# S5 input products in a two-layer hybrid encoder: two groups per weight load, against a block-diagonal operand

## The chip, the core and the metric

The kernel is one program on one core of a Trainium2 chip. The metric is device time in microseconds (us). Engines are named as in the profile: PE (TensorE's matmuls), PEld (its weight loads), DVE (VectorE), ACT (ScalarE), POOL (GpSimd), SP (the engine that issues nearly all DMAs).

## The reference

`x` is [1, 256, 1024] in float32. Each of two layers runs a half-step FFN, a mixer of three gated branches, and another half-step FFN. The change lies in the S5 branch of the mixer. Cut to that:

```
u = (h @ w_in)[..., :512]          # 256 tokens, 32 groups of 16 channels
b_bar = ((lam_bar - 1) / lam) * b  # complex, [group, 64 states, 16 channels]
bu = einsum('blgh,gph->blgp', u, b_bar)
states = scan(a*s + bu), forward and, with its own tables, backward
y = real(einsum('blgp,ghp->blgh', states, c)) + d_skip * u
y_s5 = gelu(y) * sigmoid(gelu(y) @ w_glu)
```

The other two branches are gated linear attention (GLA) and grouped-query attention. Their weighted sum goes through `w_out` and is added to `x`.

## The kernel before

**The large products.** Every weight matrix streams through `load` and `stream`: SP brings 256 rows by 512 columns (`raw`), ACT casts them to a high part (`hi`, L209), DVE subtracts to get the low part (`lo`, L210), and PE does three products per tile of 128 by 128 activations (`mm3`, L219 to L221, each 512 columns wide, tile `mm`). Four `hi` and four `lo` buffers rotate, so ACT and DVE may run at most that far ahead of PE.

**S5.** The recurrence is worked over chunks of four tokens, so 256 tokens are 64 chunks, and a group's operand for one chunk has 4 x 16 = 64 rows. `s5` transposes `u` into `U` (L797, L798): 128 partitions hold two groups, one on partitions 0 to 63 and one on 64 to 127, and there are 16 such pairs of 64 columns. It then goes through four quarters `q` of eight groups (four pairs). For each quarter: 16 input products `S` (L818), one for each pair `a`, real or imaginary part `r`, and group `g` of the pair; eight DVE products of `S` with the rotations `e` (the loop over `g` behind L818, through `mul`, L349); one addition and one subtraction; four scans into `run` (L835, L836); products back; and the output products `yp` (L853 on `U` and `mt`, L856 on the states). A float32 matmul that isn't a transpose leaves two records in the trace, one `mm` leaves one. The input product of group `g` uses only 64 rows of the array, the lower or the upper ones, and a stationary tile `bb` of 64 x 128.

**Who sets the order.** `weave` emits steps of the main stream (`w_in`, then merge gates `g0` to `g2`, GLU `G`, branch products `b0` to `b2`, `w_out`) with steps of S5, GLA and attention between them. The scheduler then puts each engine's instructions in an order of its own, by a simulated timeline. Engines run their lists in that order. The S5 work of layer 0 lies at about 240 to 375 us of the span, that of layer 1 at about 925 to 1060 us.

**Names at the far end of the mixer.** `as` (L1070) are attention scores, `apt` (L1085) transposed probabilities, `ao` (L1092) the product with the values; `amx` (L1075) is the row maximum on DVE, L1078 the exponential on ACT, L1081 the scaling on DVE. `sp`, `kv`, `go`, `goT`, `keT` belong to GLA.

Of the kernel before, what the change touches and what calls it, by code (L numbers as in the profile page):

```python
# [9 lines left out]
F32 = mybir.dt.float32  # L10
# [28 lines left out]
# main steps before a side part begins, and its steps per main step  # L39
# [12 lines left out]
# columns of the constants: those for the mixer, then those for the tables  # L52
# [4 lines left out]
def constants():  # L57
    """Arrays that depend on shapes alone, one row per partition."""
    c = np.zeros((P, C_ALL), np.float32)
    p = np.arange(P)  # L60
    inv = (10000.0 ** (-np.arange(16, dtype=np.float32) * 2.0 / 32)).astype(np.float32)
    for t in range(NT):
        tok = t * P + p
        for blk, pos in ((0, tok // 64), (1, tok % 64)):
            ang = (pos.astype(np.float32)[:, None] * inv[None]).astype(np.float64)
            for half in range(2):
                o = t * 64 + blk * 32 + half * 16
                c[:, C_COS + o:C_COS + o + 16] = np.cos(ang)
                c[:, C_SIN + o:C_SIN + o + 16] = np.sin(ang) * (1 if half else -1)
    c[:, C_MASK:C_MASK + P] = p[:, None] < p[None]  # L70
    c[:, C_TWO:C_TWO + P] = 1 + np.eye(P)
    i = np.arange(SEQ)
    c[:, C_RST:C_RST + SEQ] = i % P != 0
    n = np.arange(64)
    c[:64, C_RM:C_RM + 64] = n != 0
    c[64:, C_RM:C_RM + 64] = n != 63
    q = p % 32
    c[p, C_DM + q] = 1.0
    c[:, C_SGN] = np.where(p < 64, 1.0, -1.0)
    return c  # L80


def cols(*parts):
    """Columns of weights [K, N] side by side: for the k tiles [a, z)."""
    def f(a, z):
        res, o = [], 0
        for w, cs in parts:
            res.append((w[a * P:z * P, cs].rearrange("(k p) n -> p k n", p=P), 0, o))
            o += cs.stop - cs.start
        return res  # L90
    return f


def weave(main, sides, up=nullcontext):
    """Emit main; from its step `start` on, `per` steps of a side part after each step of main.
    sides: list of [start, per, generator]. Whatever is left of them comes in the end."""
    acc = [0.0] * len(sides)
    for i, _ in enumerate(main):
        for j, (start, per, g) in enumerate(sides):
            if i >= start:  # L100
                acc[j] += per
                while acc[j] >= 1.0:
                    acc[j] -= 1.0
                    with up():
                        next(g, None)
    for _, _, g in sides:
        for _ in g:
            pass


def rest(*gens):
    """Emit what is left of these parts, in turn, as one step."""
# [13 lines left out]
class Enc:  # L126
# [38 lines left out]
    def vectors(self, *names, eng=None):  # L165
        """Parameters of channels, to partitions: [128 channels, (layer, tile)]"""
# [26 lines left out]
    def load(self, pieces):  # L193
        """pieces: list of (dram AP [partitions, k tiles, columns], first partition, first column)"""
# [21 lines left out]
    def mm3(self, ps, act, w, first, last):  # L216
        """act: (hi, lo) [128 k, 128 tok]; w: (hi, lo) [128 k, n]"""
# [5 lines left out]
    def stream(self, act, nk, blocks, lead=1):  # L223
        """act(k, t) -> (hi, lo). blocks: list of (pieces(k0, k1) in k tiles, width, evac(t, ps)).
        The first `lead` blocks take their first chunks together."""
# [135 lines left out]
    def cmul_steps(self, o_re, o_im, a_re, a_im, b_re, b_im, tmp, neg=False):  # L361
        """o = a * b; with neg, o_im is its negative. tmp: four scratch APs"""
# [13 lines left out]
    def horner(self, out, x, cs):  # L376
        """cs from the highest power down"""
# [6 lines left out]
    def reduce_arg(self, r, n, x, inv, parts):  # L384
        """n = nearest integer of x * inv; r = x - n * (sum of parts)"""
# [40 lines left out]
    def s5_params(self, l, c):  # L426
# [68 lines left out]
        # the first four powers, turned back by a chunk  # L495
# [12 lines left out]
        # ef: powers 0 .. 7 of the turn over a chunk; eg: those of its eighth power  # L508
# [130 lines left out]
    def small_tables(self, l, pp):  # L639
        """What the mixer needs apart from its large weights: half the GLA gain, the padded gate weights with the  # L640
        bias as a last row, the rotary tables with the gains of q and k"""
# [36 lines left out]
    def split_into(self, hi, lo, src):  # L678
        """src -> two float32r parts"""
# [68 lines left out]
    def gate_stream(self, l, i, act, rstd, gates):  # L748
        """The tanh of half the gate's argument: sigmoid(v) = (1 + tanh(v / 2)) / 2"""
# [32 lines left out]
    def s5(self, l, m):  # L782
# [7 lines left out]
        U = mp.tile([P, 16, 64], F32, name=f"U{l}", tag="U")  # L790
        run = mp.tile([P, 2, GQ * 64], F32, name=f"run{l}", tag="yT")
        edge = run.rearrange("p r (g c) -> p r g c", g=GQ)
        for a in range(2):
# [4 lines left out]
            nc.scalar.copy(U[:, a * 8:a * 8 + 8], pt)  # L798
        yield
        yg = mp.tile([P, 2, 4, 8, 16], F32, name=f"yg{l}", tag="yg")  # L800
        for q in range(NQ):
# [11 lines left out]
            S = [self.psm.tile([P, 2, 256], F32, name=self.nm("S"), tag="sm") for _ in range(2)]  # L813
            for a in range(4):
                for r in range(2):
                    for g in range(2):
                        rows = slice(g * 64, (g + 1) * 64)
                        nc.tensor.matmul(S[g][:, r, a * 64:(a + 1) * 64], bb[rows, a, r], U[rows, pair[a]],  # L818
                                         start=True, stop=True)
            yield  # L820
            flat = lambda a: a.rearrange("p g c -> p (g c)")
            t1, t2, t3, t4 = (self.t2([P, 512]) for _ in range(4))
            for g in range(2):
                cs = slice(g * 256, (g + 1) * 256)
                self.mul(t1[:, cs], e[:, 0, cs], S[g][:, 0])
                self.mul(t2[:, cs], e[:, 1, cs], S[g][:, 1])
                self.mul(t3[:, cs], e[:, 0, cs], S[g][:, 1])
                self.mul(t4[:, cs], e[:, 1, cs], S[g][:, 0])
                yield
# [3 lines left out]
            # sums up to the chunk before (forward: after), nothing at the ends  # L833
# [14 lines left out]
            for i in range(2):  # L848
                gh = [(g, h, h * 2 + i, yp[g][h * 64:(h + 1) * 64, i].rearrange("p t f -> p (t f)"))
                      for g in range(2) for h in range(2)]  # L850
                for g, h, a, o in gh:
                    rows = slice(g * 64, g * 64 + 64)
                    nc.tensor.matmul(o, U[rows, pair[a]], mt[rows, a], start=True, stop=False)  # L853
# [47 lines left out]
    # ---- gate logits: z in two parts against weights in two parts, the products one above the other:  # L901
    # ---- [high z, 1 | high z, 1 | low z] . [high w, high b | low w, low b | high w]
# [18 lines left out]
    # ---- gated linear attention, both directions, a head at a time, over chunks of 128 tokens; the exponents  # L921
# [1 line left out]
    def gla(self, l, m, y):  # L923
# [26 lines left out]
        for h in range(GH):  # L950
# [34 lines left out]
            # a token's own score is the same both ways: forward ones above the diagonal, twice those on it, backward below  # L985
# [113 lines left out]
    def branch(self, l, b, y, gates):  # L1099
        """Generator bodies run late: y[b] is there by then."""  # L1100
# [76 lines left out]
```

## Time and profile before

| | |
|---|---|
| median of 3 timed runs | 1378.79 us (1378.58 to 1380.41) |
| span of the profiled execution | 1376.2 us |
| median less that span | 2.6 us |
| PE busy | 1336.0 us, 97% |
| PEld busy | 1061.6 us, 77% |
| DVE busy | 1018.4 us, 74% |
| ACT busy | 698.6 us, 51% |
| POOL busy | 73.5 us, 5% |

The page gives the profiled execution by its span, from the first to the last instruction; a timed run has a little around it. A matmul's record runs until its result has drained, so neighbouring records overlap: what a matmul costs the stream is read as the distance from its start to the start of the next. The weight loads (PEld) lie beside the matmuls. The clock of TensorE was granted in full for nearly the whole span (mean 0.996).

### The profile page before, as it was taken

Reading aid. Unit: us, or ns where it says so; the run is one execution under the profiler, and the core shown is the slowest. Engines: PE = TensorE matmul, PEld = TensorE weight load, DVE = VectorE, ACT = ScalarE, POOL = GpSimd, SP = SyncE. Lnnn points to the kernel's source line nnn. Section 1 sums busy time; section 2 is a strip of 40 time slices with the busy share of each in tenths; the row PEclk is TensorE's granted clock in tenths of the full one; section 3 lists DMA queues with packets and bytes.
Section 4 is the critical chain, followed back from the end, with each engine's and each line's share of the span. In section 5 each row is a group of like instructions: output and inputs, shape, how many; then the busy total and the mean of one; then the engine's idle time right before and its main releaser. Section 6 shows DMA issues by size and latency. Waiting matters only on the chain.

```text
span 1376.2 us, 19506 instructions
## 1 busy us (share of the span) xinstructions
PE 1336.0 (97%) x6920; PEld 1061.6 (77%) x6920; DVE 1018.4 (74%) x1826; ACT 698.6 (51%) x1102; POOL 73.5 (5%) x104
## 2 busy tenths in 40 slices
PE   7999999999999999999999999999999999999997
PEld 5878788778787678768877777887787877888886
DVE  5899975779986789996465775457799767655553
ACT  5545345447585355445355454354475754555542
POOL 1020210000100000110000000000001000000000
PEclk9999999999999999999999999999999999999999
DMA  7766666565453366666665646566654533655662
GB/s 227 195 211 224 234 222 179 189 205 198 140 183 122 107 161 206 200 202 221 198 195 173 204 149 204 180 178 202 196 200 134 168 107 122 191 178 186 182 213 76
DMA packets 201201, 249.88 MB, mean 182 GB/s; under 512 B 40856, under 2 KB 134600, under 8 KB 201104
## 3 DMA queue, kind: packets, MB, share of 16 engines
q1 hardware_dynamic: 200496, 247.59, 57.5%
q8 instruction: 54, 0.88, 0.3%
q10 hardware_dynamic: 608, 1.06, 0.2%
q14 instruction: 43, 0.35, 0.1%
HBM read 234.44 MB, written 13.11 MB: 180 GB/s over the span
## 4 chain that ended last, share of the span: by engine, by line
PE 63%; issue 17%; DVE 13%; DMA 3%; ACT 3%; POOL 1%; SPq 0%; POOLq 0%; ACTq 0%; DVEq 0%
PE mm L220 18%; PE mm L219 17%; PE mm L221 17%; DVE lo L210 4%; PE S L818 1%; DMA raw<-in_ffn_w_gate 1%; DMA raw<-in_ffn_w_up 1%; PE as L1070 1%; ACT hi L209 1%; PE ao L1092 1%; DVE t L349 1%; PE st L298 1%; DVE run L836 1%; DVE run L835 1%; PE apt L1085 1%
## 5 line engine op out<-in xcount | busy, mean ns | idle before, releaser
L210 DVE TENSOR_TENSOR lo<-raw,hi 128x1024 fp32r<-128x1024 f32 x412 | 499.4, 1217 | 191.7 <-ACT hi L209 184.1
L209 ACT CAST hi<-raw 128x1024 fp32r<-128x1024 f32 x412 | 427.7, 1042 | 305.6 <-PE mm L221 276.3
L220 PE MATMUL mm<-lo,hTh 128*128 128x512 f32 (+1 forms) x1120 | 445.3, 398 | 5.3 <-DVE lo L210 4.9
L219 PE MATMUL mm<-hi,hTh 128*128 128x512 f32 (+1 forms) x1120 | 437.6, 396 | 2.7 <-ACT hTh L267 2.7
L221 PE MATMUL mm<-hi,hTl 128*128 128x512 f32 (+1 forms) x1120 | 436.1, 392 | 0.0
L220 PEld LDWEIGHTS mm<-lo,hTh 128*128 128x128 f32 x1120 | 211.2, 189 | 51.7 <-DVE lo L210 9.2
L219 PEld LDWEIGHTS mm<-hi,hTh 128*128 128x128 f32 x1120 | 211.2, 189 | 45.5 <-ACT hTh L267 3.8
L221 PEld LDWEIGHTS mm<-hi,hTl 128*128 128x128 f32 x1120 | 210.6, 188 | 40.6 <-DVE hTl L268 0.3
L220 PE MATMUL mm<-lo,sThffn 128*128 128x512 f32 x352 | 138.9, 395 | 2.0 <-DVE lo L210 2.0
L221 PE MATMUL mm<-hi,sTlffn 128*128 128x512 f32 x352 | 138.1, 393 | 0.0
L219 PE MATMUL mm<-hi,sThffn 128*128 128x512 f32 x352 | 136.4, 395 | 0.0
L300 ACT CAST sThffn<-st 128x256 fp32r<-128x256 f32 x88 | 32.6, 372 | 128.7 <-PE st L298 128.5
L220 PEld LDWEIGHTS mm<-lo,sThffn 128*128 128x128 f32 x352 | 66.4, 189 | 16.6 <-DVE lo L210 2.5
L221 PEld LDWEIGHTS mm<-hi,sTlffn 128*128 128x128 f32 x352 | 66.5, 189 | 14.1
L219 PEld LDWEIGHTS mm<-hi,sThffn 128*128 128x128 f32 x352 | 66.5, 189 | 13.8
L301 DVE TENSOR_TENSOR sTlffn<-st,sThffn 128x256 fp32r<-128x256 f32 x88 | 36.9, 421 | 50.3 <-ACT sThffn L300 49.9
L294 ACT ACTIVATE t<-mm,rstd 128x256 f32<-128x256 f32 x88 | 41.6, 475 | 43.0 <-PE mm L221 40.2
L295 DVE SCALAR_TENSOR_TENSOR t<-mm,rstd,t 128x256 f32<-128x256 f32 x88 | 41.4, 479 | 12.6 <-ACT t L294 12.4
L818 PEld LDWEIGHTS S<-U,bb 64*128 64x128 f32 x256 | 24.6, 187 | 12.8 <-issue 11.2
L298 PE MATMUL st<-ident,t 128*128 128x128 f32 x176 | 33.4, 272 | 0.0
L298 PEld LDWEIGHTS st<-ident,t 128*128 128x128 f32 x176 | 24.4, 140 | 11.3
L349 DVE TENSOR_TENSOR t<-e,S 128x256 f32<-128x256 f32 x64 | 22.4, 414 | 12.7 <-DMA e<-scr 6.9
(355 smaller groups left out, 1452.6 us busy)
## 6 DMA issues: line engine op xcount, KB each, us to landing
raw<-in_ffn_w_gate SPq DMA_DIRECT2D x176, 256.0 KB, 3.7
raw<-in_ffn_w_up SPq DMA_DIRECT2D x176, 256.0 KB, 4.4
raw<-in_ffn_w_down SPq DMA_DIRECT2D x88, 512.0 KB, 4.6
raw<-in_w_in SPq DMA_DIRECT2D x48, 512.0 KB, 4.4
raw<-in_w_merge_gate SPq DMA_DIRECT2D x48, 512.0 KB, 3.8
raw<-in_w_out SPq DMA_DIRECT2D x16, 512.0 KB, 4.6
scr<-e SPq DMA_DIRECT2D x6, 768.0 KB, 3.7
e<-scr SPq DMA_DIRECT2D x6, 768.0 KB, 5.7
```

The source lines that it names most:

```text
L209: nc.scalar.copy(hi[:, :e - s, :width], raw[:, :e - s, :width])
L210: nc.vector.tensor_tensor(lo[:, :e - s, :width], raw[:, :e - s, :width], hi[:, :e - s, :width].bitcast(F32), op=ALU.subtract)
L219: nc.tensor.matmul(ps, act[0], w[0], start=first, stop=False)
L220: nc.tensor.matmul(ps, act[0], w[1], start=False, stop=False)
L221: nc.tensor.matmul(ps, act[1], w[0], start=False, stop=last)
L294: nc.scalar.activation(sg, ps[:, :256], AF.Silu, scale=rstd[:, t:t + 1])
L295: nc.vector.scalar_tensor_tensor(s, ps[:, 256:], rstd[:, t:t + 1], sg, op0=ALU.mult, op1=ALU.mult)
L298: nc.tensor.transpose(pt[:, j], s[:, j * P:(j + 1) * P], self.ident)
L300: nc.scalar.copy(h, pt)
L301: nc.vector.tensor_tensor(sl[:, 2 * b:2 * b + 2, t * P:(t + 1) * P], pt, h.bitcast(F32), op=ALU.subtract)
L349: self.nc.vector.tensor_tensor(out, a, b, op=ALU.mult)
L818: nc.tensor.matmul(S[g][:, r, a * 64:(a + 1) * 64], bb[rows, a, r], U[rows, pair[a]], start=True, stop=True)
```

## The change

`U` becomes a tile of 16 x 2 x 64 columns. For each pair, column block 0 holds the lower group's operand on partitions 0 to 63 and zeros below it, block 1 the upper group's operand on partitions 64 to 127 and zeros above it. POOL writes the zeros (two instructions per layer); ACT copies each transposed half to its block (four copies per layer in the place of two). One input product now uses all 128 rows and streams 128 columns: 8 products per quarter in the place of 16. `S` is split by real and imaginary part instead of by group, so that DVE takes 512 columns in one instruction, four instructions per quarter in the place of eight. The first output product (L855 now) reads its group's block of `U`. The block of SBUF that the program reserves for descriptors written by GpSimd shrinks from the default to 1024 bytes per partition; the profile before shows no queue of that kind. Comments and docstrings are taken out, some replaced by blank lines; from the S5 function on, line numbers are larger by two or three.

```diff
-        U = mp.tile([P, 16, 64], F32, name=f"U{l}", tag="U")
+        U = mp.tile([P, 16, 2, 64], F32, name=f"U{l}", tag="U")
+        for g in range(2):
+            nc.gpsimd.memset(U[g * 64:(g + 1) * 64, :, 1 - g], 0.0)
...
-            nc.scalar.copy(U[:, a * 8:a * 8 + 8], pt)
+            for g in range(2):
+                nc.scalar.copy(U[g * 64:(g + 1) * 64, a * 8:a * 8 + 8, g], pt[g * 64:(g + 1) * 64])
...
-            S = [self.psm.tile([P, 2, 256], F32, name=self.nm("S"), tag="sm") for _ in range(2)]
-            for a in range(4):
-                for r in range(2):
-                    for g in range(2):
-                        rows = slice(g * 64, (g + 1) * 64)
-                        nc.tensor.matmul(S[g][:, r, a * 64:(a + 1) * 64], bb[rows, a, r], U[rows, pair[a]],
-                                         start=True, stop=True)
+            S = [self.psm.tile([P, 4, 2, 64], F32, name=self.nm("S"), tag="sm") for _ in range(2)]
+            for r in range(2):
+                for a in range(4):
+                    nc.tensor.matmul(S[r][:, a].rearrange("p g c -> p (g c)"), bb[:, a, r],
+                                     U[:, pair[a]].rearrange("p g c -> p (g c)"), start=True, stop=True)
...
-            for g in range(2):
-                cs = slice(g * 256, (g + 1) * 256)
-                self.mul(t1[:, cs], e[:, 0, cs], S[g][:, 0])
-                self.mul(t2[:, cs], e[:, 1, cs], S[g][:, 1])
-                self.mul(t3[:, cs], e[:, 0, cs], S[g][:, 1])
-                self.mul(t4[:, cs], e[:, 1, cs], S[g][:, 0])
-                yield
+            gac = lambda x: x.rearrange("p (g a c) -> p g a c", g=2, a=4)
+            Sv = [x.rearrange("p a g c -> p g a c") for x in S]
+            self.mul(gac(t1), gac(e[:, 0]), Sv[0])
+            self.mul(gac(t4), gac(e[:, 1]), Sv[0])
+            yield
+            self.mul(gac(t2), gac(e[:, 1]), Sv[1])
+            self.mul(gac(t3), gac(e[:, 0]), Sv[1])
+            yield
...
-                    nc.tensor.matmul(o, U[rows, pair[a]], mt[rows, a], start=True, stop=False)
+                    nc.tensor.matmul(o, U[rows, pair[a], g], mt[rows, a], start=True, stop=False)
...
-    nc = bacc.Bacc("TRN2", target_bir_lowering=False, num_devices=1)
+    nc = bacc.Bacc("TRN2", target_bir_lowering=False, num_devices=1, dynamic_dma_scratch_size=1024)
```

The scheduler orders everything from the first mixer on anew. On PE, at the second quarter of layer 0, before the change the products of the lower group (`S_2819`) stand alone between the `mm` of `w_in`:

```order
L219 MATMUL mm_2754<-hi_2839,hTh_2363 128x512
L818 MATMUL S_2819<-U_2588,bb_2811 128x64
L220 MATMUL mm_2754<-lo_2840,hTh_2363 128x512
L221 MATMUL mm_2754<-hi_2839,hTl_2364 128x512
L818 MATMUL S_2819<-U_2588,bb_2811 128x64
L219 MATMUL mm_2755<-hi_2839,hTh_2363 128x512
L220 MATMUL mm_2755<-lo_2840,hTh_2363 128x512
L818 MATMUL S_2819<-U_2588,bb_2811 128x64
```

On PE at the same quarter after the change, the four products of the real part (`S_2811`) stand together:

```order
L219 MATMUL mm_2747<-hi_2823,hTh_2363 128x512
L820 MATMUL S_2811<-U_2588,bb_2803 128x128 x4
L220 MATMUL mm_2747<-lo_2824,hTh_2363 128x512
L221 MATMUL mm_2747<-hi_2823,hTl_2364 128x512
L219 MATMUL mm_2746<-hi_2829,hTh_2363 128x512
```

Counted over both layers, the input products stand in 44 runs before (16, eight single ones, 8, eight single ones, 3, 1, 4 and 16 in each layer) and in 22 after (8, 4, 4, four single ones, 2, two single ones and 8 in each layer); the single ones after are in the third quarter.

On PE at the end of attention in layer 0, before the change `mm` stand ahead of and behind this group of attention and GLA products:

```order
L221 MATMUL mm_4559<-hi_4555,ygl_3109 128x512
L1092 MATMUL ao_4225<-t_4100,av_2415 64x256
L1085 MATMUL apt_4165<-ident,t_4159 128x128 x4
L1001 MATMUL go_4151<-gst_4145,t_3966 128x128
L1000 MATMUL go_4151<-v_2419,t_3977 128x128
L1001 MATMUL go_4151<-gst_4145,t_3966 128x128
L1070 MATMUL as_4232<-akT_3542,aqT_3541 128x256 x2
L1092 MATMUL ao_4225<-t_4170,av_2415 64x256
L1092 MATMUL ao_4225<-t_4100,av_2415 64x256
L1092 MATMUL ao_4225<-t_4170,av_2415 64x256
```

After the change the same group has two more rounds of scores and probabilities ahead of it with no `mm` among them; these rows are from its middle:

```order
L1094 MATMUL ao_4029<-t_3972,av_2415 64x256
L995 MATMUL kv_4102<-v_2419,la_3078 128x128 x2
L1087 MATMUL apt_4051<-ident,t_4045 128x128 x4
L1002 MATMUL go_4107<-v_2419,t_3933 128x128
L1003 MATMUL go_4107<-gst_4101,t_3922 128x128
L1002 MATMUL go_4107<-v_2419,t_3933 128x128
L1003 MATMUL go_4107<-gst_4101,t_3922 128x128
L1094 MATMUL ao_4181<-t_4056,av_2415 64x256
L1072 MATMUL as_4188<-akT_3498,aqT_3497 128x256 x2
L1087 MATMUL apt_4121<-ident,t_4115 128x128 x4
```

Four groups of `apt` follow each other here without an `mm` between them; before, two.

## Rows read from the trace of the kernel before

**Rows 1.** The page: span; busy time, share of the span, instructions.

```profile
span 1376.2 us, 19506 instructions
...
PE 1336.0 (97%) x6920; PEld 1061.6 (77%) x6920; DVE 1018.4 (74%) x1826; ACT 698.6 (51%) x1102; POOL 73.5 (5%) x104
```

**Rows 2.** Busy time by stretch: stretch, PE, PEld, DVE, ACT, POOL, clock, DMA.

```profile
250.00:320.00 70.00, 70.00 (x418) 52.38 (x417) 54.83 (x81) 29.55 (x41) 0.54 (x2) 1.00 0.57 185
320.00:400.00 80.00, 77.17 (x463) 62.49 (x462) 78.56 (x135) 56.06 (x109) 7.55 (x4) 1.00 0.54 176
...
933.00:1003.00 70.00, 70.00 (x418) 52.29 (x417) 54.68 (x81) 29.64 (x41) 0.54 (x2) 1.00 0.57 185
```

**Rows 3.** PE in order of time, layer 0: start, length, instructions (two records per product).

```profile
250.22 2.00 PE L818 MATMUL S<-U,bb 64*128 64x64 f32 x32
252.16 1.09 PE L714 MATMUL qkT<-ident,t 128*128 128x128 f32 x8
...
260.18 0.50 PE L220 MATMUL mm<-lo,hTh 128*128 128x512 f32 x1
260.52 0.39 PE L221 MATMUL mm<-hi,hTl 128*128 128x512 f32 x1
260.84 0.43 PE L818 MATMUL S<-U,bb 64*128 64x64 f32 x2
261.20 0.50 PE L219 MATMUL mm<-hi,hTh 128*128 128x512 f32 x1
...
277.78 2.00 PE L818 MATMUL S<-U,bb 64*128 64x64 f32 x16
279.70 0.50 PE L221 MATMUL mm<-hi,hTl 128*128 128x512 f32 x1
```

**Rows 4.** PE in order of time, GLA products of 128 x 128 among the `mm`.

```profile
441.60 0.39 PE L221 MATMUL mm<-hi,ygl 128*128 128x512 f32 x1
441.83 0.60 PE L993 MATMUL kv<-v,la 128*128 128x128 f32 x4
442.19 0.48 PE L219 MATMUL mm<-hi,ygh 128*128 128x512 f32 x1
442.50 0.40 PE L220 MATMUL mm<-lo,ygh 128*128 128x512 f32 x1
```

**Rows 5.** Line 349 (DVE): duration ns min/median/max, first and last start us, shapes.

```profile
L349 DVE TENSOR_TENSOR t<-e,S x64: 409/414/422, 252.3 to 1032.8; 128x256 f32<-128x256 f32 x64
L349 DVE TENSOR_TENSOR t<-e,run x32: 677/685/693, 262.5 to 1052.8; 128x512 f32<-128x512 f32 x32
...
L349 DVE TENSOR_TENSOR t<-qk,sa x16: 207/308/411, 377.3 to 1070.9; 128x256 f32<-128x256 f32 x8, 128x64 f32<-128x64 f32 x8
```

**Rows 6.** What DVE waited for, 250 to 320 us: us, times, longest.

```profile
DVE lo L210 <- ACT hi L209: 9.6, 6, 2.8
...
DVE t L349 <- PE S L818: 2.8, 2, 2.6
```

**Rows 7.** Line 798 (ACT): the copies to `U`.

```profile
L798 ACT COPY U<-uT x4: 586/588/590, 245.1 to 928.6; 128x512 f32<-128x512 f32 x4
```

**Rows 8.** Line 649: a POOL memset of 1024 columns.

```profile
L649 POOL MEMSET wraw<- x2: 948/952/957, 0.9 to 481.1; 96x1024 f32 x2
```

**Rows 9.** DVE by line, 430 to 460 us: busy, mean ns, idle before.

```profile
L1075 DVE TENSOR_REDUCE amx<-as 128x2 f32<-128x512 f32 x4 | 2.8, 688 | 0.4 <-PE as L1070 0.4
L1081 DVE TENSOR_SCALAR t<-t,asm 128x256 f32<-128x256 f32 x8 | 2.5, 349 | 0.1
```

**Rows 10.** ACT by line, the same stretch.

```profile
L1078 ACT ACTIVATE t<-as,amx 128x256 f32<-128x256 f32 x8 | 3.7, 478 | 0.0
...
L1078 ACT ACTIVATION_READ_ACCUMULATOR t<-as,amx 128x1 f32 x8 | 1.7, 207 | 0.0
```

**Rows 11.** PE at the two groups of `apt` that follow each other without an `mm`.

```profile
448.88 0.30 PE L1014 MATMUL goT<-ident,t 128*128 128x128 f32 x1 [0.23 <-DVE t L1011]
...
450.71 0.72 PE L1085 MATMUL apt<-ident,t 128*128 128x128 f32 x4 [0.21 <-DVE t L1081]
```

More of the change, by code (lines that the diff above doesn't have):

```diff
@@ L812, in s5 @@
             pair = [(j // 2) * 8 + q * 2 + j % 2 for j in range(4)]
-            S = [self.psm.tile([P, 2, 256], F32, name=self.nm("S"), tag="sm") for _ in range(2)]
-            for a in range(4):
-                for r in range(2):
-                    for g in range(2):
-                        rows = slice(g * 64, (g + 1) * 64)
-                        nc.tensor.matmul(S[g][:, r, a * 64:(a + 1) * 64], bb[rows, a, r], U[rows, pair[a]],
-                                         start=True, stop=True)
+            S = [self.psm.tile([P, 4, 2, 64], F32, name=self.nm("S"), tag="sm") for _ in range(2)]
[3 more added lines that the diff above has]
+                                     U[:, pair[a]].rearrange("p g c -> p (g c)"), start=True, stop=True)
             yield
-            flat = lambda a: a.rearrange("p g c -> p (g c)")
             t1, t2, t3, t4 = (self.t2([P, 512]) for _ in range(4))
-            for g in range(2):
-                cs = slice(g * 256, (g + 1) * 256)
-                self.mul(t1[:, cs], e[:, 0, cs], S[g][:, 0])
-                self.mul(t2[:, cs], e[:, 1, cs], S[g][:, 1])
-                self.mul(t3[:, cs], e[:, 0, cs], S[g][:, 1])
-                self.mul(t4[:, cs], e[:, 1, cs], S[g][:, 0])
-                yield
+            gac = lambda x: x.rearrange("p (g a c) -> p g a c", g=2, a=4)
[6 more added lines that the diff above has]
+            yield
             self.add(t1, t1, t2)
```

## Prediction

> **What bounds the kernel now.** I read the page's busy times first. PE is busy for 1336.0 us of the span of 1376.2 us, DVE for 1018.4, ACT for 698.6 [rows 1]. PE is thus the bound over the whole, and what its stream no longer has to do is time, wherever no other engine is late. Next I read the busy times by stretch around S5 in layer 0. From 250 to 320 us PE is busy all 70.0 us and DVE 54.83; from 320 to 400 us PE is busy 77.17 of 80 and DVE 78.56 [rows 2]. So first PE alone decides, then PE and DVE run nearly level, and DVE has no room. Layer 1 repeats it 683 us later almost to the digit: 70.00 and 54.68 in the stretch that answers to the first [rows 2]. I work out one layer and double it.
>
> Then I read PE in order of time, to see what an input product costs the stream. The distance between the starts of neighbouring `mm` is 0.23 us (441.60 to 441.83) [rows 4]. Where the scheduler has put one product alone between `mm`, the start of one `mm` pair at 260.18 and of the next at 261.20 are 1.02 us apart, with two `mm` and one product between [rows 3]. Less 2 x 0.23, one lone product costs 0.56 us. Its two records are a small part of that: the `mm` ahead takes 0.32 us to the next start (260.52 to 260.84) where 0.23 is usual, and the `mm` behind 0.34 (260.18 to 260.52). Passing from a product of 64 rows to one of 128 rows and back costs about 0.2 us beside the product's own 0.36. Where 16 products stand together, with lower and upper group in turn, all of them take 1.94 us (250.22 to 252.16), 0.12 each [rows 3]. Where eight of one group stand together they take 1.92 us (277.78 to 279.70), 0.24 each [rows 3]. The price of a product is set by its neighbours.
>
> **The change on PE.** Products of 128 rows and 128 columns in plain float32 are there already, in GLA: four records stand between `mm` from 441.83 to 442.19, and the `mm` behind them takes 0.31 us in the place of 0.23 [rows 4]. That is 0.44 us for four records, 0.11 a record, and no more for the passage. A new product has two records, 0.22 us, and does the work of two old ones.
>
> By quarter, in layer 0, with the runs of the order in the section on the change:
> - First quarter, 16 together: 1.94 us, and about 0.2 for its one passage. After: 8 x 0.22 = 1.8. Saved 0.3.
> - Second quarter, eight alone and eight of one group together: 8 x 0.56 + 1.92 + 0.2 = 6.6. After: 1.8. Saved 4.8.
> - Third quarter, 16 products in 11 runs (eight single ones, 3, 1, 4): I price it as the second, since the singles are as many and the rest is cut up more, partly by other products that don't fill the array. Saved 4.8.
> - Fourth quarter, 16 together: saved 0.3, as the first.
>
> Sum 10.2 us a layer, 20.4 in all. Its lower bound is 2 x 5.4 = 10.8, if the third quarter's singles cost only what packed products do because their neighbours pay the passage anyway. Its upper bound is about 25, since the new order also has `as` in fewer, longer runs and I count nothing for that.
>
> **The change on DVE.** Before, 32 products of 256 columns a layer at 0.414 us, 13.2 us. After, 16 of 512 columns; the row of that width is 0.685 us [rows 5], 11.0 us. Saved 2.2 a layer. The new ones read `S` in runs of 64 elements with two groups interleaved; the row of products on the query tile, which go by runs of 16, needs at most 0.411 us for 256 columns [rows 5], no more than a plain one, so I add nothing. Were the order of reading dear, the ends are 0.685 us and 2 x 0.414, which gives between 2.2 and 0 a layer. The larger instruction waits for four products of one part and not for eight of one group; these come sooner.
>
> **The change on ACT and POOL.** ACT gets four copies to `U` at 0.588 us [rows 7] in the place of two (half the partitions, as many columns each): 1.2 us more a layer. They stand ahead of `hi` casts in ACT's queue, and ACT is busy 29.55 of these 70 us [rows 2]; cost nothing, and at worst 1.2 us where a cast is late. POOL's two memsets of 1024 columns take about 0.95 us each, by the row of that length [rows 8], and stand ahead of the root of the norm (L277) in POOL's queue. What covers them is that POOL is idle there and the root is wanted only by the first evacuation of `w_in`, a hundred `mm` later; without cover 1.9 us a layer. The zeros cost PE nothing beside the wider stream, which is in the 0.22. The smaller descriptor block I cost at nothing.
>
> **What of it reaches the end.** Saved before 320 us: 0.3 + 4.8 + 4.8 = 9.9 us. DVE must then do its 54.83 us of that stretch, less 1.7 for three quarters, in 60.1 us and not 70. Of its 15.2 us of idle time there, 9.6 are waits of `lo` for `hi` and 2.8 are waits for `S` [rows 6]: both follow PE, since `hi` waits for a buffer that PE frees. They shrink as PE speeds up. DVE would be at 88%, below the 98% at which it runs from 320 us on [rows 2]. But it enters that second stretch with fewer `lo` ahead, and there PE can be held by DVE. I take off 1.9 us for that, and the fourth quarter's 0.3 counts for nothing where DVE is level: 8.0 us a layer reach the end, 16 in all.
>
> Against the profiled span: 1376.2 - 16 = 1360.2 us. The median of the timed runs lies 2.6 us above the span, so 1362.8 us is forecast.
>
> **Rivals.**
> 1. DVE is the real bound over both stretches. Then all that PE saves comes back as waits for `lo` between 320 and 400 us, and the gain is DVE's own 2 x 2.2 = 4.4: 1374.4 us. For it speaks DVE's 78.56 of 80; against it that in the stretch before DVE's idle is PE's doing. Chance 0.17.
> 2. The change does nothing on PE. Two products on different halves of the array run at the same time; one of 128 columns with half zeros does the same work in the same time. The packed run says so: 2 x 0.12 against 0.22 [rows 3, 4]. If the lone products were hidden behind something I don't see, the rest would follow it: 1378.8 us, within 0.2%. Against it stand the 1.02 us of [rows 3]. Chance 0.08. The Trainium skill has this as a rule in TensorE: Matmul & The Clock Gate, Part 3 (packing small matmuls): small-K matmuls whose operands lie on different row groups run concurrently, and the gain of packing is just that. By it the sum on PE would be 0; the trace agrees in the runs of 16 and not for products of one group or lone ones, where nothing stands beside them in the other half.
> 3. Slower: the end of attention runs dry. In the new order four groups of `apt` follow each other without an `mm`, where two did. Between scores and `apt` lie the maximum (0.688), two exponentials with their read-outs (2 x (0.478 + 0.207)) and two scalings (2 x 0.349) [rows 9, 10]: 2.8 us in series. If PE waits all of it four times, that is 11 us a layer, 22 in all, and 1362.8 + 22 = 1385 us. It makes the kernel slower from 8 us a layer on. Against it: at the two unfilled groups of before PE waited 0.23 and 0.21 us [rows 11], because scores of the next head are issued ahead. Chance 0.09.
>
> **Chances.** The forecast has 0.66, by itself from 1354 to 1370: 20.4 with a little of the upper bound at one end, half of it at the other. The range must take in the first rival and most of the second, and leaves out the third and the far upper end: 1353 to 1377 us. A change under 0.2% (2.8 us, so above 1376.0) can't be told from none by such runs. Faster: the forecast's 0.66 and 0.15 of the first rival, 0.81. Same: the second's 0.08, the first's 0.02 and 0.01 of the third, 0.11. Slower: 0.08.
>
> **What would show it.** Line 820 has 128 records of about 0.11 us each, with `mm` at 0.23 us right up to them; PE's busy time falls by some 16 to 20 us. DVE's products of `S` are 32 at about 0.685 us. The stretch from the first input product to the fourth quarter is shorter by about 10 us, and DVE's waits for `hi` in it fall from 9.6 to a few us. Wrong would be: PE idle ahead of `mm` L220 for `lo` of 8 us and more a layer (first rival); records of the new product far over 0.11 us or `mm` at 0.32 beside them (second); idle time ahead of `apt` of some us each (third).

## The result, and the profile after

The changed kernel takes 1359.18 us (median of 4 runs, 1357.79 to 1361.01) against 1378.68 for the kernel before in the same session (1378.24 to 1380.41): a ratio of 0.9855, 95% interval 0.9841 to 0.9868. It is faster by 19.5 us; 16 were forecast, and the forecast of 1362.8 lies 3.6 us above the measurement.

The page after, to be held against [rows 1]:

```profile
span 1356.0 us, 19228 instructions
...
PE 1310.3 (97%) x6792; PEld 1049.8 (77%) x6792; DVE 1013.2 (75%) x1794; ACT 703.5 (52%) x1106; POOL 76.9 (6%) x108
```

PE is busy for 25.7 us less, where the prediction looked for 16 to 20, and still for 97% of a span that is 20.2 us shorter. ACT and POOL have some us more, as the added copies and zeros want.

Busy time by stretch, with the columns of [rows 2]; the first stretch is taken 10 us shorter than there, by about what the prediction has saved in it:

```profile
250.00:310.00 60.00, 59.68 (x369) 47.71 (x368) 50.12 (x63) 28.52 (x40) 0.54 (x2) 1.00 0.67 216
310.00:390.00 80.00, 76.69 (x441) 61.98 (x440) 78.29 (x125) 55.11 (x100) 6.47 (x4) 1.00 0.57 183
925.00:985.00 60.00, 60.00 (x371) 48.25 (x370) 50.84 (x64) 29.69 (x41) 0.54 (x2) 1.00 0.67 221
```

The picture is the same as before: PE full in the first stretch, PE and DVE level in the second. DVE's share of the first rose from 78% to 84%.

PE in order of time, first and second quarter of layer 0, to be held against [rows 3]:

```profile
249.75 1.95 PE L820 MATMUL S<-U,bb 128*128 128x128 f32 x16
251.53 1.04 PE L714 MATMUL qkT<-ident,t 128*128 128x128 f32 x8
...
259.74 0.39 PE L219 MATMUL mm<-hi,hTh 128*128 128x512 f32 x1
259.96 1.05 PE L820 MATMUL S<-U,bb 128*128 128x128 f32 x8
260.77 0.48 PE L220 MATMUL mm<-lo,hTh 128*128 128x512 f32 x1
261.09 0.39 PE L221 MATMUL mm<-hi,hTl 128*128 128x512 f32 x1
```

Eight products take 1.78 us (249.75 to 251.53), 0.22 each. Four of them among `mm` take 0.81 us; the `mm` ahead is not disturbed (0.22 us, 259.74 to 259.96), the one behind takes 0.32 instead of 0.23.

DVE's products of `S`, against [rows 5], and ACT's and POOL's new instructions, against [rows 7, 8] (duration ns min/median/max, first and last start):

```profile
L349 DVE TENSOR_TENSOR t<-e,S x32: 677/682/690, 251.2 to 1017.4; 128x512 f32<-128x512 f32 x32
...
L802 ACT COPY U<-uT x8: 580/582/588, 244.2 to 921.5; 64x512 f32<-64x512 f32 x8
...
L793 POOL MEMSET U<- x4: 945/947/948, 215.8 to 892.5; 64x1024 f32 x4
```

What DVE waited for from 250 to 320 us (us, times, longest), first the kernel before (the line that stands between those of [rows 6]), then after:

```profile
DVE t L349 <- DMA e<-scr: 3.2, 1, 3.2
```

```profile
DVE t L349 <- DMA e<-scr: 9.3, 2, 5.1
DVE lo L210 <- ACT hi L209: 1.1, 1, 1.1
```

The waits of `lo` for `hi` fell from 9.6 to 1.1 us, and those for `S` are gone. In their place DVE waits for the table `e`, which has one buffer: the next quarter's table can be fetched only when this quarter's last reader is done. No step of the prediction speaks of that wait.

Landmarks of PE's timeline, worked out from its rows (us):

| | before | after |
|---|---|---|
| layer 0, `U`'s transposes to first `mT` (the mixer) | 244.3 to 470.1: 225.8 | 243.5 to 460.3: 216.8 |
| layer 1, the same | 927.4 to 1153.2: 225.8 | 919.0 to 1133.1: 214.1 |

And the mixer's PE time by kind, as distances from each start to the next, with what goes beyond 0.45 us counted as a gap (before, then after in layer 0 and layer 1): input products 13.8, 6.4 and 6.3; what `mm` take beyond 0.23 us each 9.5, 7.5 and 6.9; scores `as` 8.2, 6.4 and 6.4; GLU 6.6, 5.7 and 5.7; `apt` 3.0, 4.5 and 4.5; gaps 2.7, 5.2 and 3.8. The first two are where the change acts: 9.4 and 10.1 us a layer, though `mm` also pay for their other small neighbours. The others come with the new order: 2.7 us won at the scores and GLU, 1.5 and 1.4 lost at `apt`, 2.5 and 1.1 lost in gaps; the rest, 0.9 and 1.3 us less, is spread over smaller kinds. PE's order is the same in both layers after the change, so the 2.7 us by which the two mixers differ are not the order's. Most of them are waits between 300 and 366 us.

### The profile page after: what moved, and what is told of

Same layout as the page of the kernel before. It is cut to its first block, busy times and chain, and to the rows that moved or that the text cites. A ratio compares the mean times of both kernels' runs of the same rounds, so it can differ in the third digit from the quotient of the medians.

```text
span 1356.0 us, 19228 instructions
## 1 busy us (share of the span) xinstructions
PE 1310.3 (97%) x6792; PEld 1049.8 (77%) x6792; DVE 1013.2 (75%) x1794; ACT 703.5 (52%) x1106; POOL 76.9 (6%) x108
## 4 chain that ended last, share of the span: by engine, by line
PE 58%; issue 18%; DVE 17%; DMA 4%; ACT 3%; POOL 1%; SPq 0%; POOLq 0%; ACTq 0%; DVEq 0%
PE mm L220 17%; PE mm L219 16%; PE mm L221 16%; DVE lo L210 5%; DVE t L349 2%; DMA raw<-in_ffn_w_gate 1%; DVE run L838 1%; DMA e<-scr 1%; PE as L1072 1%; PE ao L1094 1%; DVE run L837 1%; PE st L298 1%; ACT hi L209 1%; DMA raw<-in_ffn_w_up 1%; PE pt L263 1%
## 5 line engine op out<-in xcount | busy, mean ns | idle before, releaser
L349 DVE TENSOR_TENSOR t<-e,S 128x512 f32<-128x512 f32 x32 | 20.2, 683 | 17.3 <-DMA e<-scr 17.2
L627 POOL COPY kx<-ks 128x128 f32<-128x128 f32 x32 | 18.9, 630 | 218.7 <-DVE ks L610 218.7
```

Of the source, the lines that this page charges most:

```text
L349: self.nc.vector.tensor_tensor(out, a, b, op=ALU.mult)
L627: nc.gpsimd.tensor_copy(kx[:, :, s], ks.rearrange("p g j f -> p g (j f)")[:, :, (3 - s) * 16:(3 - s) * 16 + 64])
```

## The experiments

All were timed in turn with the kernel before; the ratios are against it, with 95% intervals. Differences from the changed kernel are those of the medians, against its 1359.18 us; where the intervals of two ratios overlap, a difference is not taken as shown. A trace is of one execution. PE's list is the same in all these kernels up to the first input products, and yet `U`'s transposes start anywhere from 243.3 to 247.8 us in their traces; so two spans that differ by some us say little, and distances inside a mixer are read instead.

**Is it the neighbours that make a 64-row product dear?** The kernel before, with the order of one quarter's products on PE held as written, so that lower and upper halves alternate:

```diff
-                        nc.tensor.matmul(S[g][:, r, a * 64:(a + 1) * 64], bb[rows, a, r], U[rows, pair[a]],
-                                         start=True, stop=True)
+                        ins = nc.tensor.matmul(S[g][:, r, a * 64:(a + 1) * 64], bb[rows, a, r], U[rows, pair[a]],
+                                               start=True, stop=True)
+                        if a + r + g:
+                            self.tc.keep_in_program_order(ins)
```

> The kernel before, with its 64-row products, its operand U without zeros and its narrow DVE products; only the order on PE is bound: within a quarter each input product stands behind the one before it, lower and upper half in turn, so that a layer has 8 runs (16, 1, 15, 1, 5, 2, 8, 16) in the place of 22. Theory (the price of a product is set by its neighbours: a lone one 0.56 us, one with its partner 0.12 us): the products cost about 2.1 + 2.6 + 3.0 + 2.1 = 9.8 us a layer against 17.2 before, 15 us saved in all on PE, of which 11 to 15 reach the end: 1364 to 1368 us. Rival A (only the wide, zero-padded product is cheap): 1377 to 1380 us. Rival B (the gain is DVE's fewer instructions): 1377 to 1380 us.

1371.12 us (1369.86 to 1373.7), ratio 0.9946 [0.9931, 0.996]: 7.5 us gained where 11 to 15 were expected. PE in order of time at the second quarter:

```profile
260.41 0.50 PE L219 MATMUL mm<-hi,hTh 128*128 128x512 f32 x1
260.85 0.43 PE L818 MATMUL S<-U,bb 64*128 64x64 f32 x2
261.21 0.50 PE L220 MATMUL mm<-lo,hTh 128*128 128x512 f32 x1
...
275.89 2.00 PE L818 MATMUL S<-U,bb 64*128 64x64 f32 x30
277.81 0.50 PE L220 MATMUL mm<-lo,hTh 128*128 128x512 f32 x1
```

Fifteen products take 1.92 us, 0.13 each, where eight of one half took as long [rows 3]; the one that still stands alone costs what it did. Input products fall from 13.8 to 8.7 us a layer, and layer 0's mixer by 7.5 us, the most that the expectation has for one layer. Layer 1's mixer grew by 1.0: PE has 7.7 us of gaps there, and the clock column falls (busy time by stretch, columns as before):

```profile
1025.00:1065.00 40.00, 38.03 (x210) 30.64 (x210) 37.96 (x63) 22.18 (x47) 9.82 (x2) 0.96 0.52 172
1065.00:1105.00 40.00, 36.12 (x225) 29.95 (x223) 33.01 (x67) 27.82 (x61) 3.84 (x2) 0.91 0.36 113
```

This trace is of the slowest of the four executions (1373.70 us), so part of layer 1's loss may be its own. The price by neighbours holds, and neither rival of the expectation does; what happens elsewhere in the mixers, by the new order or by waits, is as large as half the effect.

**Is it filled rows, or fewer products?** The changed kernel with every product issued twice, so that the number of products and their runs are those of before (16, eight single ones, 8, ...) while the array does twice the work of after:

```diff
-                for a in range(4):
+                for a in (0, 1, 2, 3, 0, 1, 2, 3):
```

> The changed kernel with each input product issued twice into the same place (the second overwrites with the same values): as many products as before the change, 128, and by the built order in the same kind of runs (16, eight single ones, 8, nine single ones, 4, 3, 16 in each layer), but on all 128 rows and 128 columns wide. Theory: two records of 0.11 us each and no passage, so 64 x 0.22 = 14 us more on PE, of which 11 to 14 reach the end: 1370 to 1374 us. Rival A (any plain float32 product alone among the mm costs 0.56 us): 0.34 us more for some 34 single ones, 1381 to 1386 us. Rival B (DVE is the bound, PE has room): 1359 to 1363 us.

1365.86 us (1364.99 to 1368.25), ratio 0.9908 [0.9893, 0.9923]: 6.7 us slower than the change alone, where 11 to 14 were expected, and still 12.8 faster than before. The products cost nearly what the theory says, 6.5 us a layer more on PE, but only half of it reaches the end. PE at the second quarter, where the products stand alone as they did before:

```profile
262.53 0.39 PE L220 MATMUL mm<-lo,hTh 128*128 128x512 f32 x1
262.76 0.38 PE L820 MATMUL S<-U,bb 128*128 128x128 f32 x2
262.90 0.48 PE L221 MATMUL mm<-hi,hTl 128*128 128x512 f32 x1
263.22 0.38 PE L820 MATMUL S<-U,bb 128*128 128x128 f32 x2
263.36 0.48 PE L219 MATMUL mm<-hi,hTh 128*128 128x512 f32 x1
```

One `mm` and one lone product take 0.46 us (262.76 to 263.22): less the `mm`'s 0.23, the product costs 0.23. Before, a lone product with half the rows and half the columns cost 0.56 [rows 3]. For this product the filled rows decide, not the work. The second rival, by which 128 columns with half zeros are no gain, is refuted at the lone products. The Trainium skill's TensorE: Matmul & The Clock Gate, Part 3, has small-K matmuls on different row groups run concurrently; the trace agrees where the other half stands next (0.13 us against 0.24), and shows beside it a price of standing alone that the rule doesn't have.

The kernel before has other small products among `mm`, and they show that it isn't the rows alone (`go` has a stationary tile of 128 rows and 128 columns, `ao` one of 128 rows and 64 columns):

```profile
442.97 0.39 PE L219 MATMUL mm<-hi,ygh 128*128 128x512 f32 x1
443.21 0.38 PE L1000 MATMUL go<-v,t 128*128 128x128 f32 x2
443.34 0.48 PE L220 MATMUL mm<-lo,ygh 128*128 128x512 f32 x1
...
444.36 0.39 PE L221 MATMUL mm<-hi,ygl 128*128 128x512 f32 x1
444.68 0.65 PE L1092 MATMUL ao<-t,av 128*64 128x256 f32 x2
```

The `mm` ahead of `go` takes 0.24 us, the one ahead of `ao` 0.32, as ahead of the old input products, though `ao` fills all rows. What is dear in these traces is a tile that leaves half of the array free, by rows or by columns.

**Does DVE's wider instruction matter?** The changed kernel with DVE's products 256 columns wide, eight a quarter, as before:

```diff
+            for g in range(2):
+                cs = slice(g * 256, (g + 1) * 256)
+                ac = lambda x: x[:, cs].rearrange("p (a c) -> p a c", a=4)
+                self.mul(ac(t1), ac(e[:, 0]), S[0][:, :, g])
...
```

> The changed kernel, but DVE takes the products of S 256 columns at a time again, 32 a layer at about 0.41 us, 2.2 us more a layer. Theory (PE's stream is what was shortened): DVE has room for three of the four quarters, so 1359 to 1362 us. Rival (DVE is the bound over the whole of S5): all 4.4 us come back, 1363.6 us or more.

1364.36 us (1361.81 to 1365.46), ratio 0.9897 [0.988, 0.9913]: 5.2 us slower than the change. That is the rival's result, not the theory's (1359 to 1362), and as much as DVE's products lose (64 x 0.416 - 32 x 0.682 = 4.8 us), as if DVE's time counted in full, though it is idle for a quarter of the span. The mixers take 218.0 and 218.1 us. But the order changed too, and `half_muls` below takes 11 us of work off DVE and gains nothing; so the equality isn't proof of where each us went.

**How much does a mere redrawing do?** Two runs. The first swaps the two loops around the product, the same work in another order:

```diff
-            for r in range(2):
-                for a in range(4):
+            for a in range(4):
+                for r in range(2):
```

> The changed kernel with the two loops around the input product exchanged (pair outside, part inside): the same instructions on every engine, with the same work in each; the scheduler's order comes out anew from the first mixer on. Theory: what is gained is in the instructions, so within 3 us of the changed kernel, 1356 to 1362 us. Rival (a good part of the gain is a lucky order): 1364 us or more.

1360.83 us (1359.3 to 1361.28), ratio 0.9864 [0.9849, 0.9879]: no difference from the change, as expected. The second is the kernel before with the smaller descriptor block alone (`dynamic_dma_scratch_size=1024`), the order unchanged:

> The kernel before with nothing but the smaller descriptor block; the order of the instructions on every engine is that of before, and only the tiles' addresses move. Theory: no change, 1377 to 1380 us. Rival (the addresses or the block are part of the gain): 1375 us or less.

1379.84 us (median of 10 runs, 1376.7 to 1386.32), ratio 1.001 [0.9995, 1.0024]: nothing, as the prediction costed it.

**What bounds the kernel now?** Four kernels that leave out work of the changed one, to see which engine's time still counts. First PE's: the imaginary part's products are left out.

```diff
-            S = [self.psm.tile([P, 4, 2, 64], F32, name=self.nm("S"), tag="sm") for _ in range(2)]
-            for r in range(2):
+            S = [self.psm.tile([P, 4, 2, 64], F32, name=self.nm("S"), tag="sm")] * 2
+            for r in range(1):
```

> The changed kernel without the input products of the imaginary part (32 of 64 left out; DVE reads the real part's in their place, so the result of S5 is another). PE has 32 x 0.22 = 7 us less work. Twice the products gave 13 us more records and 6.7 us more time, about half. Theory (PE and DVE are nearly level in S5, so PE work counts by half): 1355 to 1357 us. Rival A (PE alone is the bound): 1351 to 1353 us. Rival B (after the change DVE alone is the bound): 1358.5 to 1360 us.

1358.06 us (1357.25 to 1359.84), ratio 0.9847 [0.9833, 0.9862]: no difference, where 2 to 4 us were expected, with 3.5 us less of input products a layer. PE's gaps grew to 6 to 7 us a mixer. Then DVE's: two of the four products of `S`.

```diff
             self.mul(gac(t1), gac(e[:, 0]), Sv[0])
-            self.mul(gac(t4), gac(e[:, 1]), Sv[0])
             yield
-            self.mul(gac(t2), gac(e[:, 1]), Sv[1])
             self.mul(gac(t3), gac(e[:, 0]), Sv[1])
...
```

The sum, the difference and the scans then take the two products that are left.

> The changed kernel without two of the four DVE products of S in each quarter (the sums take the other two twice, so the result of S5 is another): 16 instructions less at 0.68 us, 11 us less DVE work over both layers, all else as it was. Theory (level engines, with PE a little ahead as the bound): a third to a half of it shows, 1353.5 to 1356 us. Rival A (PE alone is the bound): 1358 to 1360 us. Rival B (DVE alone): 1348 to 1350 us.

1358.75 us (1356.29 to 1359.86), ratio 0.9848 [0.9834, 0.9863]: no difference either, where 3 to 6 us were expected, though S5's last product starts 12.7 to 15.2 us earlier. With neither alone worth anything, both might be level, so both were left out together (the two edits above):

> The changed kernel with both pieces left out at once: the input products of the imaginary part (7 us of PE work) and two of the four DVE products of S in each quarter (11 us of DVE work); the result of S5 is another. Alone they gave 1.1 and 0.4 us. Theory (after the change PE and DVE are level over the mixer, so relief of one is taken up by the other): together they give far more than the sum, 4 to 8 us, 1351 to 1355 us. Rival (a third thing bounds the mixer, such as the chain through scans and tables): 1356.5 to 1359 us.

1362.45 us (1361.51 to 1367.71), ratio 0.988 [0.9861, 0.9899]: 3.3 us above the change with all its work (the intervals overlap a little), where some us below were expected. My theory of level engines, that each hides what is taken from the other, fell by this run. The trace, which is of the slowest of the four executions (1367.71 us, 5.3 above the median), shows a way (DVE in order of time, then PE):

```profile
277.39 1.28 DVE L349 TENSOR_TENSOR t<-e,S 128x512 f32<-128x512 f32 x2 [5.49 <-DMA e<-scr]
278.70 0.69 DVE L352 TENSOR_TENSOR t<-t,t 128x512 f32<-128x512 f32 x1
...
283.63 1.22 DVE L836 TENSOR_TENSOR_SCAN run<-e,t 64x511 f32<-64x511 f32 x1
284.88 2.36 DVE L210 TENSOR_TENSOR lo<-raw,hi 128x1024 fp32r<-128x1024 f32 x2
```

```profile
282.68 0.27 PE L917 MATMUL zTp<-ident,t 128*96 128x128 f32 x1
286.16 0.69 PE L220 MATMUL mm<-lo,hTh 128*128 128x512 f32 x1 [3.21 <-DVE lo L210]
286.65 0.63 PE L221 MATMUL mm<-hi,hTl 128*128 128x512 f32 x1
287.07 0.63 PE L219 MATMUL mm<-hi,hTh 128*128 128x512 f32 x1
...
289.63 0.44 PE L220 MATMUL mm<-lo,hTh 128*128 128x512 f32 x1
289.91 0.39 PE L221 MATMUL mm<-hi,hTl 128*128 128x512 f32 x1
```

DVE waits 5.49 us for the table `e`. Its list is fixed, so the sums and four scans behind that product come next, and `lo` only after them, at 284.88. PE stands still for `lo` at 282.95 and starts its next `mm` at 286.16; from there to 289.63 `mm` are 0.43 us apart on average and soon 0.23 again.

The wait for `e` was taken away in both kernels by a second buffer:

```diff
-        return {name: self.ld.tile([P, z - a], F32, name=self.nm(name), tag="s5" + name) for name, (a, z) in SCR_AT.items()}
+        return {name: self.ld.tile([P, z - a], F32, name=self.nm(name), tag="s5" + name, bufs=1 + (name == "e")) for name, (a, z) in SCR_AT.items()}
```

In the changed kernel, with all its work:

> The changed kernel with two buffers for the rotations e in the place of one, so that the next quarter's are brought while this quarter's are in use. In the changed kernel DVE waits 9.3 us in 250 to 310 us of layer 0 for that transfer, 3.2 us before the change. Theory (this wait has taken the place of the waits for hi, and the DVE time lost there is missing in the level stretch behind it): the wait falls under 2 us and 2 to 5 us are gained over both layers, 1354 to 1357 us. Rival (DVE's idle time there costs nothing because PE is the bound): 1358 to 1361 us.

1358.3 us (1357.75 to 1359.27), ratio 0.9851 [0.9836, 0.9866]: no difference. DVE's waits from 250 to 310 us are now

```profile
DVE lo L210 <- ACT hi L209: 3.5, 3, 1.4
DVE t L349 <- PE S L820: 1.7, 2, 0.9
```

so the 9.3 us for `e` are gone and cost the changed kernel nothing that the medians can tell. That doesn't exclude a small price: the mixers of this trace take 213.8 us each, against 216.8 and 214.1, and intervals of this width would hide a gain of 2 us. In the kernel with both halves left out:

> As half_both (the changed kernel without the imaginary part's products and without two of the four products of S on VectorE in each quarter), with two buffers for the table e, so that the next quarter's table can be on its way while the last is still read. What is left out is the same as in half_both. Theory, the wait for the table e is what ate the saving of half_both: DVE's 5.5 us of waiting for e go, lo is not late behind it, TensorE's 3.2 us of waiting for lo at the second quarter go, and the time falls by 5 us or more, to 1350 to 1357 us. Rival, the order as a whole and the engines' being level late in the mixer decide: the wait for e goes and TensorE waits elsewhere instead, 1358 to 1363 us, within 3 us of the changed kernel.

1356.56 us (1356.1 to 1358.27), ratio 0.9837 [0.9821, 0.9854]: 5.9 us faster than the same without the second buffer (the intervals don't overlap), at the theory's edge of 5 us and in its 1350 to 1357. Here DVE's waits are

```profile
DVE lo L210 <- ACT hi L209: 3.0, 3, 1.1
DVE t L349 <- PE S L820: 2.1, 1, 2.1
```

and PE's gaps fall from 6.7 to 3.6 us in layer 0's mixer and from 6.7 to 3.2 in layer 1's, together about as much as the medians differ by. So the second buffer is worth 5.9 us in that kernel, and the wait for `e` is the likely cause; the order was redrawn by it too, so the share of the wait isn't shown apart. But 1356.56 is no more than 2.6 us under the change, with intervals that overlap, and 3.4 us a layer less of input products. By PE's distances the order gave the rest back in each layer: `mm` beyond 0.23 us 1.1 to 1.3 more than after, `as` 1.0, `go` 0.8, GLU 0.6. Why the scheduler's order comes out so was not tried.

**Do longer runs of scores pay?** The changed kernel, with the scores `as` of the two halves of the array held in turn:

```diff
-                    nc.tensor.matmul(sps[v][:, t], aqT[rows, j, t * P:(t + 1) * P], akT[rows, j // 2], start=True, stop=True)
+                    ins = nc.tensor.matmul(sps[v][:, t], aqT[rows, j, t * P:(t + 1) * P], akT[rows, j // 2],
+                                           start=True, stop=True)
+                    if t + v:
+                        self.tc.keep_in_program_order(ins)
```

> The changed kernel, and the four attention scores of a pair of heads bound to stand in their written order, lower and upper half of the array in turn, where two of one half stood together. Theory (halves in turn run beside each other): a run of four costs about 1.2 us in the place of two runs of about 1.2, 4 us a layer on PE at a place where DVE has room (30 of 40 us busy); 1352 to 1356 us. Rival (that stretch is bound by the chain from scores to probabilities and not by PE): 1357 to 1361 us.

1362.65 us (1361.8 to 1365.65), ratio 0.9877 [0.986, 0.9893]: 3.5 us slower at the medians, though the intervals overlap a little; no gain in any case, and outside both theory (1352 to 1356) and rival (1357 to 1361). The scores take 0.5 us a layer less, where 4 were expected, and PE's waits from 395 to 445 us (us, times, longest) show part of what stands against it, first the change, then this kernel:

```profile
PE keT L980 <- ACT aqT L1060: 1.1, 1, 1.1
PE ao L1094 <- ACT t L1089: 0.7, 1, 0.7
PE goT L1016 <- DVE t L1013: 0.5, 1, 0.5
```

```profile
PE ao L1097 <- ACT t L1092: 2.0, 3, 0.7
PE keT L980 <- ACT aqT L1060: 1.1, 1, 1.1
PE mm L219 <- ACT ygh L680: 0.5, 1, 0.5
```

Last, that kernel with S5's first sum and difference moved from DVE to POOL:

```diff
-            self.add(t1, t1, t2)
-            self.sub(t3, t3, t4)
+            nc.gpsimd.tensor_tensor(t1, t1, t2, op=ALU.add)
+            nc.gpsimd.tensor_tensor(t3, t3, t4, op=ALU.subtract)
```

> The scores in turn as in the run beside it, and the first sum and difference of each quarter of S5 on POOL in the place of DVE: 4.4 us less DVE work a layer at 0.55 us each; the profile before has POOL at 2.1 us for a product of 512 columns, so S5's own chain is 3 us longer a quarter. Theory of level engines: with PE relieved too, 1 to 4 us under the run beside it. Rival (the longer chain, or POOL in DVE's way): 0 to 6 us over it.

1373.05 us (1372.48 to 1374.77), ratio 0.9951 [0.9936, 0.9966]: 10.4 us slower than the kernel it starts from, more than the rival had. POOL and DVE in order of time, then POOL's two lines:

```profile
256.20 1.29 POOL L833 TENSOR_TENSOR t<-t,t 128x512 f32<-128x512 f32 x1
...
256.28 2.29 DVE L837 TENSOR_TENSOR_SCAN run<-e,t 64x511 f32<-64x511 f32 x1 [0.87 <-POOL t L832]
258.58 1.22 DVE L838 TENSOR_TENSOR_SCAN run<-e,t 64x511 f32<-64x511 f32 x1
...
L832 POOL TENSOR_TENSOR t<-t,t x8: 1282/1290/1301, 255.0 to 1025.7; 128x512 f32<-128x512 f32 x8
...
L833 POOL TENSOR_TENSOR t<-t,t x8: 1287/1783/2279, 256.2 to 1026.9; 128x512 f32<-128x512 f32 x8
```

The sum takes 1.29 us where DVE takes 0.69. The first scan waits for the sum alone and starts while POOL still works at the difference; in six of the eight quarters it then takes 2.28 to 2.29 us instead of 1.21. Of the 8.8 us that DVE was to save over both layers, 6.5 go in these scans: POOL stands in DVE's way, the second half of the rival. What makes up all 10.4 us isn't worked out; the mixers take 223.0 and 221.8 us against 218.5 and 216.5, and PE is busy only 57.06 of the 60 us from 250 to 310.

## Why the prediction was right, step by step

- **What bounds.** Right up to this change: PE is at 97% before and after, and what PE's stream lost came off the time. Beyond it no longer: 3.5 us a layer less on PE gained nothing in `half_products`.
- **The price of a product.** Right. 0.22 us for a new product in a run, and nothing but the usual 0.09 in the `mm` behind it; alone 0.23 in all, where the old one cost 0.56. `halves_in_turn` and `products_twice` show the two sides of it (the prediction calls the two records a small part of the 0.56, but by its own rows they are 0.36 of it): the same 64-row products are cheap when the other half stands next, and padded to the full array they are cheap alone.
- **The sum on PE.** Right in size. 10.2 us a layer predicted, 9.4 and 10.1 measured on the products and `mm` together. What the upper bound allowed for, that "the new order also has `as` in fewer, longer runs", came to 1.8 a layer, and 0.9 more at GLU. One sign of it failed: from the first input product to the fourth quarter it is not 10 us less but 3.5 and 4.6 (92.2 us before; 88.8 and 87.6 after), since the new order puts 293 `mm` in that stretch instead of 274. Counted to the same `mm`, about the 200th behind `U`'s transposes, PE is 10.7 and 11.2 us ahead.
- **DVE.** The instruction is 0.682 us (0.685 predicted); reading `S` interleaved costs nothing.
- **ACT and POOL.** The copies and memsets have the predicted durations, and PE runs without a gap from `U`'s transposes to the first input product (243.50 to 249.75), so neither was late. Cost nothing, as said.
- **What reaches the end.** This is the term that was mis-sized: 8.0 us a layer, where 9.0 and 11.7 were measured from `U` to `mT`. The two make 20.7; 0.8 more lies ahead of `U`'s transposes, where PE's list is the same before and after, the stretch between the mixers loses 1.4, and with 0.1 at the end that is the span's 20.2. I had taken 1.9 off for DVE holding PE after 320 us, a number with no row behind it, and had counted nothing for the scores and GLU. PE did wait for `lo` (2.9 and 1.8 us a layer, 0.8 before in layer 0), but beside the products and their `mm` the rest of the mixer lost only 0.3 us in layer 0 and won 1.6 in layer 1. That the forecast came within 3.6 us is thus in part luck: gains and losses that it did not count nearly cancel.
- **DVE's waits.** Those for `hi` fell "to a few us", to 1.1. That the table `e` would be late next I missed: 3.2 became 9.3 us. Taking it away gained nothing measurable here, and 5.9 us in the kernel with less work.
- **The first rival** (DVE the real bound) is wrong as a whole, since the gain isn't 4.4; but in `narrow_dve` going back on DVE's part of the change costs 5.2 us, new order included. If the three parts are taken to add up, an estimate from the medians, filled rows give 7.6 us (12.8 of `products_twice` less 5.2), half the number of products 6.7 and DVE's width 5.2. That they add up isn't shown. `halves_in_turn` reached 7.5 on its own road.
- **The third rival** (attention's end runs dry) is there in small: PE's waits of 0.5 to 1.1 us quoted above, where it needed 11 us a layer. The group of `apt` without an `mm` was covered by `ao` and `as` between.

What stays open is why nothing taken from PE or DVE beyond the change brings more than 3 us. The runs show that the order is redrawn by every edit but the descriptor block's, that single kinds of work move by 0.5 to 2 us a layer either way with it, and that in one case a second buffer for a table gave 5.9 us; they don't show what the best order of the same work would take.

## What to carry to other kernels

Read the price of a small matmul as the distance between its neighbours' starts, not from its record: one that fills only half of the array's rows, alone in a stream of full ones, cost 0.56 us here, and one padded with zeros to full rows 0.23. Fill the rows, or put the other half's product next to it. Where a scheduler orders all engines, test an edit of some us against a mere redrawing of the order, and look at which wait comes next in the list of the engine that you relieved: here it was a table with a single buffer. Before work is moved to an engine that is idle, look at what the others do beside it: DVE's scans took nearly twice as long next to POOL's subtraction.

## What the runs showed of the hardware that was not expected

- A lone float32 product of 128 rows and 128 columns adds 0.23 us to the stream with its passage (262.76 to 263.22 in `products_twice`, less one `mm`); the passage itself is only in the `mm` behind it (0.32 in the place of 0.23). A lone one of 64 rows lengthens the `mm` ahead too (0.32), and so does one that fills all rows and half of the array's columns (`ao`, 444.36 to 444.68 before).
- After 3.2 us in which PE waited, `mm` stood 0.43 us apart for 3.5 us (286.16 to 289.63 in `half_both`), and then 0.23: 1.2 GHz, the lower of the two levels, in the place of 2.4. Eight steps of 0.43 for 0.23 make this wait 1.6 us dearer than itself; the granted clock is 0.57 from 286 to 290 us.
- POOL's addition of 512 columns takes 1.29 us for DVE's 0.69. A scan on DVE that meets POOL's subtraction takes 2.29 us instead of 1.21 (256.28 in `scores_pool`).
